# The last product of a decoder trunk: one half of the rows finished ahead of the other, with a norm and a way out for each half

## Chip, cores and metric

The kernel runs on one core of a Trainium2 chip. The metric is device microseconds (us) of one execution, lower is better; the number for a kernel is the median of its runs.

## What is computed

A decoder trunk of two layers over 256 positions of 2048 features, all float32. Only the end bears on this case: the last feed-forward's down projection, the residual, and the final norm.

```
gu = h @ w_gu;  gate, up = gu[..., :5632], gu[..., 5632:]
x = x + (silu(gate) * up) @ w_down          # w_down: 5632 x 2048
out = x * rsqrt(mean(x * x, axis=-1) + 1e-6) * norm_final
```

The root and its reciprocal are one number for each of the 256 rows.

## The kernel before

**Weights.** All weight matrices come as one stream of blocks of 128 x 1024 float32 (512 KB), in the order of use. `emit_dma` (L122) loads a block into one of five buffers (`wraw`) from SyncE's queue. `emit_split` (L130) writes it as the sum of two float32r halves: ScalarE copies it to `whi` (L134), VectorE subtracts that from it to get `wlo` (L135); there are three buffers of each. `next_block` (L148) hands out the next block and keeps the halving up to three blocks and the loads up to five blocks ahead in the written order.

**A wide product.** `wide_gemm` (L201) multiplies 256 rows by 512 columns of weights. A block holds two chunks of 128 x 512. The rows come in two halves, t = 0 (rows 0..127) and t = 1 (rows 128..255), each with an accumulator (`acc`) of its own in PSUM. For each chunk k and each half there are three matmuls: activation high by weight high (L211), high by low (L212), low by high (L213). The down projection has 44 chunks, so 22 blocks, for each of four column groups j.

**Residual and squares.** `residual` (L693) adds the accumulator to `xs`, the resident x (L698, VectorE, 128 x 512 a half), and squares it with a row sum into `ssq` (L701, ScalarE). In the last feed-forward GpSimd multiplies the finished columns by the final norm's gain for j = 0, 1, 2 (L705); for j = 3 the gain is multiplied in at the very end.

**Final norm.** `row_scale` (L680) sums the squares of both halves together (L685), takes the root on ScalarE (L686), and on VectorE the reciprocal with one correction step (L688 to L691). Then L831 to L836 multiply the eight 128 x 512 tiles by the row factor, VectorE for t = 0 (L835) and for the last columns of both (L831), ScalarE for t = 1 (L833). Each tile goes out with a transfer of 256 KB of its own, all eight from SyncE's queue (L836).

**Tables.** ScalarE's root and Silu are in different activation tables; a table is loaded where the next function in ScalarE's order needs one that is not there. The last Silu (L735) is in the last feed-forward's gate product.

**Order.** The order of the instructions on each engine is fixed when the program is built, by a planner. It plays the program through by its own costs: an instruction becomes free to go when its inputs are there and its buffers are free, and an engine takes, of those that are free to go, the one that was written first. The code as written is therefore no list of the order on an engine.

Of the kernel before, what the change touches and what calls it, by code (L numbers as in the profile page):

```python
# [11 lines left out]
F32 = mybir.dt.float32  # L12
F32R = mybir.dt.float32r
AF = mybir.ActivationFunctionType
OP = mybir.AluOpType
AX = mybir.AxisListType

P = 128
D = 2048
S = 256  # L20
# [12 lines left out]
EPS = 1e-6  # L33
# [12 lines left out]
N5 = 512  # L46
NJ = D // N5
# [15 lines left out]
def nsa_pool_trunk(ctx, tc, xT, xn, gain0, small, band, gfin, w_kc, w_qk, w_vg, w1k, w1v, w_o,  # L63
                   p_in, p_grp, p_out, gu, down, out):
    nc = tc.nc
# [5 lines left out]
    tmp = ctx.enter_context(tc.tile_pool(name="tmp", bufs=2))  # L71
# [3 lines left out]
    RAW, SPL = 5, 3  # L75
# [62 lines left out]
    def ahead(b):  # L138
        while state["split"] < min(len(stream), b + SPL):
            while state["dma"] <= state["split"]:  # L140
                emit_dma(state["dma"])
                state["dma"] += 1
            emit_split(state["split"])
            state["split"] += 1
        while state["dma"] < min(len(stream), b + RAW):
            emit_dma(state["dma"])
            state["dma"] += 1

    def next_block():
        b = state["used"]  # L150
        ahead(b)
        state["used"] += 1
        return parts.pop(b)


    def bank(own=False):

        i = state["acc"]
        state["acc"] += 1
        if state["more"] is None or own or i % state["turn"] == 0:  # L160
            return mm.tile([P, 512], F32, name="acc")
        return state["more"].tile([P, 512], F32, name="acc")
# [35 lines left out]
                k += 1  # L198
        return ps

    def wide_gemm(rhs, own=False):  # L201

        ps = [bank(own) for _ in range(2)]
        n = len(rhs)
        for k in range(n):
            if k % 2 == 0:
                w = next_block()
            hi, lo = (a[:, k % 2 * N5:(k % 2 + 1) * N5] for a in w)
            for t in range(2):
                xa, xb = (rhs[k][:, a * S + t * P:a * S + (t + 1) * P] for a in range(2))  # L210
                nc.tensor.matmul(ps[t], xa, hi, start=k == 0, stop=False)  # L211
                nc.tensor.matmul(ps[t], xa, lo, start=False, stop=False)  # L212
                nc.tensor.matmul(ps[t], xb, hi, start=False, stop=k == n - 1)  # L213
        return ps

    def whole(ps, name):

        t = tmp.tile([P, S], F32, name=name)
        nc.scalar.activation(t, ps[:, S:], AF.Copy)
        nc.vector.tensor_tensor(t, ps[:, :S], t, op=OP.add)  # L220
        return t
# [4 lines left out]
    eps = cst.tile([P, 1], F32, name="eps")  # L226

    def col(name, i=None, p=P):
        if name == "g_mix0":
            return g0[:, i:i + 1]  # L230
        a, b = COLS[name]
        return sm[:p, a:b] if i is None else sm[:p, a + i:a + i + 1]
# [10 lines left out]
    rcol = xgp.tile([P, 2], F32, name="rcol")  # L243
# [51 lines left out]
    with tc.tile_pool(name="first", bufs=1, reuse_waits="tile") as fp, \  # L295
# [5 lines left out]
        for b, n in enumerate(KB):  # L301
            x = x2[k0 // 2]
# [19 lines left out]
        k = 0  # L322
        for n in KB:
            hi, lo = next_block()
            for i in range(n):
                for j in range(3):
                    o = (3 * i + j) * P
# [30 lines left out]
        for j in range(2):  # L358
            ps = whole(gemm2(xg), "up").rearrange("p (c i k) -> p i c k", i=CS // 2, k=2)
            f = rst.rearrange("p (c i k) -> p i c k", i=CS // 2, k=2)  # L360
            for g in range(2):
                a = slice(g * DV, (g + 1) * DV)
# [12 lines left out]
        for u in range(2):  # L375

            t = fp.tile([P, KQ, 3, G, CS], F32, name="kab", bufs=2)
            w = col("posk")[:, u * CS:(u + 1) * CS].rearrange("p (m j) -> p m j", j=4)
# [4 lines left out]
            for j in range(3):  # L383
                r = slice(32 * j, 32 * j + 32)
# [3 lines left out]
            t = t.rearrange("p m j g c -> p (m j) g c")  # L388
            kab.append(halves(t, [P, 3 * KQ, G, CS], f"kab{u}"))
            t = fp.tile([P, CS // 2, G, CS], F32, name="vab", bufs=2)  # L390
            w = col("posv")[:, u * CS // 2:(u + 1) * CS // 2]
# [6 lines left out]
        for br in range(2):  # L398
# [4 lines left out]
            for u in range(2):  # L403
                o = CS + u * S + br * P
# [104 lines left out]
    op = ctx.enter_context(ExitStack())  # L509
# [4 lines left out]
    bias = {}  # L514
# [130 lines left out]
    for q in range(NH // 4):  # L645
# [3 lines left out]
        for j in range(3):  # L649
            ps = gemm(xg)  # L650
# [3 lines left out]
        for h in range(4 * q, 4 * q + 4, 2):  # L654
# [7 lines left out]
            o = oT[h // 2]  # L662
# [5 lines left out]
    xp = ctx.enter_context(tc.tile_pool(name="xp", bufs=1, reuse_waits="tile"))  # L668
# [1 line left out]
    state["turn"] = 3  # L670
    psT = ctx.enter_context(tc.tile_pool(name="psT", bufs=2, space=bass.MemoryType.PSUM))
    xs = xp.tile([P, 2, D], F32, name="xs")
    ssq = xp.tile([P, 2, NJ], F32, name="ssq")
    for t in range(2):
        nc.sync.dma_start(xs[:, t], xn[t * P:(t + 1) * P, :])

    def turn():
        return psT.tile([P, 2 * S], F32, name="turn")

    def row_scale():  # L680

        tot = tmp.tile([P, 2], F32, name="tot")
        a = tmp.tile([P, 2], F32, name="na")
        t = tmp.tile([P, 2], F32, name="nt")
        nc.vector.tensor_reduce(tot, ssq, axis=AX.X, op=OP.add)  # L685
        nc.scalar.activation(t, tot, AF.Sqrt, scale=1.0 / D, bias=eps)  # L686
        nc.vector.tensor_scalar(a, tot, 1.0 / D, EPS, op0=OP.mult, op1=OP.add)
        nc.vector.reciprocal(rcol, t)  # L688
        nc.vector.scalar_tensor_tensor(t, rcol, -0.5, rcol, op0=OP.mult, op1=OP.mult)
        nc.vector.tensor_tensor(t, t, a, op=OP.mult)  # L690
        nc.vector.scalar_tensor_tensor(rcol, t, 1.5, rcol, op0=OP.add, op1=OP.mult)  # L691

    def residual(j, ps, gain, gf=None):  # L693


        xc = [xs[:, t, j * N5:(j + 1) * N5] for t in range(2)]
        for t in range(2):
            nc.vector.tensor_tensor(xc[t], ps[t], xc[t], op=OP.add)  # L698
        for t in range(2):
            sq = xp.tile([P, N5], F32, name="sq", bufs=2)  # L700
            nc.scalar.activation(sq, xc[t], AF.Square, accum_out=ssq[:, t, j:j + 1])  # L701
        if gf is not None:
            if j < NJ - 1:
                for t in range(2):
                    nc.gpsimd.tensor_tensor(xc[t], xc[t], gf[j], op=OP.mult)  # L705
            return
        for q in range(2):
            tr = turn()
            for i in range(2):
                for t in range(2):  # L710
                    o = (2 * q + i) * P
                    nc.tensor.transpose(tr[:, i * S + t * P:i * S + (t + 1) * P], xc[t][:, o:o + P],  # L712
                                        ident)
            for i in range(2):
                spread(4 * j + 2 * q + i, tr[:, i * S:(i + 1) * S], gain)
# [11 lines left out]
    def ffn(gain, fpool):  # L727
        hid2, hid = pairs(fpool, FT, "hid")
        for f in range(FJ):
            pg = wide_gemm(xg)  # L730
            if f == 0:
                row_scale()
            sg = [fpool.tile([P, N5], F32, name=f"sg{t}", bufs=1) for t in range(2)]
            for t in range(2):
                nc.scalar.activation(sg[t], pg[t], AF.Silu, scale=rcol[:, t:t + 1])  # L735
            pu = wide_gemm(xg)
            h = [fpool.tile([P, N5], F32, name="h", bufs=4) for t in range(2)]
            for t in range(2):
                nc.vector.scalar_tensor_tensor(h[t], pu[t], rcol[:, t:t + 1], sg[t], op0=OP.mult,
                                               op1=OP.mult)  # L740
            for q in range(2):
                tr = turn()
                for i in range(2):
                    for t in range(2):
                        o = (2 * q + i) * P
                        nc.tensor.transpose(tr[:, i * S + t * P:i * S + (t + 1) * P],  # L746
                                            h[t][:, o:o + P], ident)
                split_pair(hid2[2 * f + q], tr)
        gf = None
        if gain is None:  # L750
            gf = [fpool.tile([P, N5], F32, name="h", bufs=4) for _ in range(NJ)]
            for j in range(NJ):
                nc.sync.dma_start(gf[j], gfin[:, j * N5:(j + 1) * N5])
        for j in range(NJ):
            residual(j, wide_gemm(hid), gain, gf)
        return gf

    for j in range(NJ):
        residual(j, wide_gemm(oT, own=j == 0), "g_ffn0")
# [6 lines left out]
    with tc.tile_pool(name="pl", bufs=1, reuse_waits="tile") as pl:  # L766
# [52 lines left out]
        rhs = [mixed[4 * g + c] for g in GROUPS for c in range(4)]  # L819
# [1 line left out]
            residual(j, wide_gemm(rhs), "g_ffn1")  # L821

    with tc.tile_pool(name="f1", bufs=1, reuse_waits="tile") as fpool:
        gf = ffn(None, fpool)
        row_scale()
        for j in (*range(NJ - 1), NJ - 1):
            for t in range(2):
                o = xs[:, t, j * N5:(j + 1) * N5]
                r = rcol[:, t:t + 1]
                if j == NJ - 1:  # L830
                    nc.vector.scalar_tensor_tensor(o, o, r, gf[j], op0=OP.mult, op1=OP.mult)  # L831
                elif t:
                    nc.scalar.activation(o, o, AF.Copy, scale=r)  # L833
                else:
                    nc.vector.tensor_scalar(o, o, r, None, op0=OP.mult)  # L835
                nc.sync.dma_start(out[t * P:(t + 1) * P, j * N5:(j + 1) * N5], o)  # L836


def _buckets():
# [118 lines left out]
```

## Time and profile before

| what | value |
|---|---|
| median of 3 runs | 2144.52 us |
| lowest and highest run | 2143.55, 2146.86 us |
| the profiled execution: its own time | 2141.8 us |
| its span, first to last instruction | 2139.6 us |
| TensorE busy | 2113.2 us, 99% of the span |
| VectorE, ScalarE, GpSimd busy | 55%, 48%, 3% |
| mean granted TensorE clock | 0.998 |

The profiled execution's time stands 2.2 us above its span. Times in the rows below are microseconds from the first instruction. TensorE's last matmul starts at 2125.85 us; what comes after it is the tail that the change works on.

### The profile page before, as it was taken

How to read it: one execution, taken by the hardware profiler on the slowest of the kernel's cores; microseconds unless marked ns; L12 is line 12 of the kernel's file. 1: busy time of each engine (PE TensorE's matmuls, PEld its weight loads, DVE VectorE, ACT ScalarE, POOL GpSimd, SP SyncE). 2: the span in 40 equal slices, each digit the busy share in tenths (PEclk: the TensorE clock that was granted, in tenths of full speed). 3: DMA queues.
4: the chain of work that ended last, by engine and by line, in shares of the span. 5: the costliest groups of instructions: out<-in, count | busy, mean ns of one | idle time of the engine just before them, and what ended most of it. 6: DMA issues, size and time to landing. Idle time of an engine off the chain costs nothing.

```text
span 2139.6 us, 28065 instructions
## 1 busy us (share of the span) xinstructions
PE 2113.2 (99%) x10780; PEld 1803.5 (84%) x10780; DVE 1181.9 (55%) x1527; ACT 1035.2 (48%) x1481; POOL 73.3 (3%) x135
## 2 busy tenths in 40 slices
PE   8999999999999999999999999999999999999997
PEld 7899999888888888888888888888888888888886
DVE  7768888555554545544444555555444554444443
ACT  5667777454444444444444455444444444444443
POOL 4001111000000000000000000000000000000000
PEclk9999999999999999999999999999999999999999
DMA  7664444666666666666666656666666666666664
GB/s 235 200 218 136 146 139 136 199 180 194 190 187 188 188 194 188 186 192 192 191 193 188 198 175 184 182 191 186 189 190 193 188 187 189 192 208 195 191 194 128
DMA packets 115720, 396.91 MB, mean 186 GB/s; under 512 B 13539, under 2 KB 19939, under 8 KB 115331
## 3 DMA queue, kind: packets, MB, share of 16 engines
q1 hardware_dynamic: 115538, 395.07, 62.1%
q8 instruction: 84, 1.38, 0.3%
q14 instruction: 50, 0.40, 0.1%
q10 hardware_dynamic: 48, 0.07, 0.0%
HBM read 391.25 MB, written 2.16 MB: 184 GB/s over the span
## 4 chain that ended last, share of the span: by engine, by line
PE 93%; DVE 0%; ACT 0%; DVEq 0%; issue 0%
PE acc L212 27%; PE acc L211 27%; PE acc L213 27%; PE acc L166 2%; PE acc L168 2%; PE acc L167 2%; PE turn L746 1%; PE ps_o L639 1%; PE ps_t L601 1%; PE ps_s L535 1%; PE ps_s L533 1%; PE ps_s L534 1%; PE turn L712 0%; PE ps_o L630 0%; PE ps_o L629 0%; PE ps_o L631 0%
## 5 line engine op out<-in xcount | busy, mean ns | idle before, releaser
L135 DVE TENSOR_TENSOR wlo<-wraw,whi 128x1024 fp32r<-128x1024 f32 (+1 forms) x727 | 886.9, 1221 | 855.8 <-ACT whi L134 849.0
L134 ACT ACTIVATE whi<-wraw 128x1024 fp32r<-128x1024 f32 (+1 forms) x727 | 765.6, 1053 | 924.6 <-PE acc L213 850.1
L213 PE MATMUL acc<-whi,xg 128*128 128x512 f32 x1536 | 599.8, 390 | 0.0
L212 PE MATMUL acc<-wlo,xg 128*128 128x512 f32 x1536 | 598.3, 390 | 0.0
L211 PE MATMUL acc<-whi,xg 128*128 128x512 f32 x1536 | 545.8, 390 | 0.0
L212 PEld LDWEIGHTS acc<-wlo,xg 128*128 128x128 f32 x1536 | 288.4, 188 | 59.2
L213 PEld LDWEIGHTS acc<-whi,xg 128*128 128x128 f32 x1536 | 288.4, 188 | 59.2
L211 PEld LDWEIGHTS acc<-whi,xg 128*128 128x128 f32 x1536 | 288.5, 188 | 58.5
L212 PE MATMUL acc<-wlo,hid 128*128 128x512 f32 x704 | 274.2, 390 | 0.0
L213 PE MATMUL acc<-whi,hid 128*128 128x512 f32 x704 | 274.1, 389 | 0.0
L211 PE MATMUL acc<-whi,hid 128*128 128x512 f32 x704 | 247.4, 390 | 0.0
L212 PEld LDWEIGHTS acc<-wlo,hid 128*128 128x128 f32 x704 | 132.1, 188 | 27.4
L211 PEld LDWEIGHTS acc<-whi,hid 128*128 128x128 f32 x704 | 132.2, 188 | 27.3
L213 PEld LDWEIGHTS acc<-whi,hid 128*128 128x128 f32 x704 | 132.2, 188 | 27.1
L166 PE MATMUL acc<-xg,whi 128*128 128x256 f32 x432 | 124.3, 289 | 6.1 <-ACT whi L134 5.8
L167 PE MATMUL acc<-xg,whi 128*128 128x256 f32 x432 | 123.2, 287 | 0.0
L168 PE MATMUL acc<-xg,wlo 128*128 128x256 f32 x432 | 121.5, 288 | 0.7 <-DVE wlo L135 0.6
L166 PEld LDWEIGHTS acc<-xg,whi 128*128 128x128 f32 x432 | 82.8, 192 | 6.9 <-ACT whi L134 6.3
L167 PEld LDWEIGHTS acc<-xg,whi 128*128 128x128 f32 x432 | 83.0, 192 | 0.0
L168 PEld LDWEIGHTS acc<-xg,wlo 128*128 128x128 f32 x432 | 81.5, 192 | 1.5 <-DVE wlo L135 1.1
L561 ACT ACTIVATE prob<-prob,mx 128x128 f32<-128x128 f32 (+1 forms) x128 | 56.6, 445 | 9.8 <-DVE mx L555 6.8
L212 PE MATMUL acc<-wlo,oT 128*128 128x512 f32 x128 | 50.8, 396 | 0.0
(211 smaller groups left out, 1876.1 us busy)
## 6 DMA issues: line engine op xcount, KB each, us to landing
wraw<-in_gu SPq DMA_DIRECT2D x352, 512.0 KB, 3.7
wraw<-in_down SPq DMA_DIRECT2D x176, 512.0 KB, 3.7
wraw<-in_w_qk SPq DMA_DIRECT2D x64, 512.0 KB, 4.3
wraw<-in_w_o SPq DMA_DIRECT2D x32, 512.0 KB, 3.7
wraw<-in_p_in SPq DMA_DIRECT2D x32, 512.0 KB, 3.6
wraw<-in_p_out SPq DMA_DIRECT2D x32, 512.0 KB, 3.6
bias<-skew SPq DMA_DIRECT2D x32, 200.0 KB, 3.3
wraw<-in_p_grp SPq DMA_DIRECT2D x8, 512.0 KB, 3.8
```

Source lines behind the costliest of these rows:

```text
L134: nc.scalar.activation(hi[:, :n], t[:, :n], AF.Copy)
L135: nc.vector.tensor_tensor(lo[:, :n], t[:, :n], hi[:, :n].bitcast(F32), op=OP.subtract)
L166: nc.tensor.matmul(ps, hi, x[:, :S], start=first, stop=False)
L167: nc.tensor.matmul(ps, hi, x[:, S:], start=False, stop=False)
L168: nc.tensor.matmul(ps, lo, x[:, :S], start=False, stop=last)
L211: nc.tensor.matmul(ps[t], xa, hi, start=k == 0, stop=False)
L212: nc.tensor.matmul(ps[t], xa, lo, start=False, stop=False)
L213: nc.tensor.matmul(ps[t], xb, hi, start=False, stop=k == n - 1)
L533: nc.tensor.matmul(o, q[0], k[0], start=True, stop=False)
L534: nc.tensor.matmul(o, q[0], k[1], start=False, stop=False)
L535: nc.tensor.matmul(o, q[1], k[0], start=False, stop=True)
L561: nc.scalar.activation(p[:, o:o + n], p[:, o:o + n], AF.Exp, bias=mx[:, i:i + 1], accum_out=su[:, i:i + 1])
```

## The change

`wide_gemm` gets an argument `apart`. The last `apart` chunks are written half by half: all their matmuls for t = 0, then all for t = 1. The last product of the program (j = 3 of the last down projection) is called with `apart=6`, three blocks. Those three blocks are asked for together, before the first of the 18 matmuls of t = 0.

`residual` and `row_scale` are no longer used for that last product. A new function `finish` does the residual, the squares, the norm and the output of one half; it is written for t = 0 and then for t = 1. The residual and the squares go in two pieces of 256 columns. The sum of the first three column groups and the first piece is taken apart from the last piece, and enters the root as its bias. ScalarE multiplies columns 0..1023 by the row factor in one instruction, VectorE the rest in two. Each half goes out in two transfers of 512 KB in place of four of 256 KB; the front columns of t = 1 go from ScalarE's queue, the others from SyncE's.

Ahead of the last down projection, behind the last Silu in the code, a root of one column that nobody reads is written, `root`. Its input is `eps`, a column made at the start (L238). `ssq` gets one more column.

```diff
-        for k in range(n):
+        def step(k, w, t):
+            hi, lo = (a[:, k % 2 * N5:(k % 2 + 1) * N5] for a in w)
+            xa, xb = (rhs[k][:, a * S + t * P:a * S + (t + 1) * P] for a in range(2))
+            nc.tensor.matmul(ps[t], xa, hi, start=k == 0, stop=False)
+            nc.tensor.matmul(ps[t], xa, lo, start=False, stop=False)
+            nc.tensor.matmul(ps[t], xb, hi, start=False, stop=k == n - 1)
+
+        for k in range(n - apart):
             if k % 2 == 0:
                 w = next_block()
...
             for t in range(2):
...
+                step(k, w, t)
+        ws = [next_block() for _ in range(apart // 2)]
+        for t in range(2):
+            for k in range(n - apart, n):
+                step(k, ws[(k - n + apart) // 2], t)
...
+            nc.scalar.activation(tmp.tile([P, 1], F32, name="root"), eps, AF.Sqrt)
-        for j in range(NJ):
+        for j in range(NJ - (gf is not None)):
             residual(j, wide_gemm(hid), gain, gf)
-        return gf
+        if gf is not None:
+            ps = wide_gemm(hid, apart=2 * SPL)
+            for t in range(2):
+                finish(t, ps[t], gf[NJ - 1])
+
+    def finish(t, ps, g):
+        h = N5 // 2
+        o = D - N5
+        x = xs[:, t]
+        for i in range(2):
+            a = x[:, o + i * h:o + (i + 1) * h]
+            nc.vector.tensor_tensor(a, ps[:, i * h:(i + 1) * h], a, op=OP.add)
+            sq = xp.tile([P, N5], F32, name="sq", bufs=2)
+            nc.scalar.activation(sq[:, :h], a, AF.Square, accum_out=ssq[:, t, NJ - 1 + i:NJ + i])
+        part, a, r, u = (xp.tile([P, 1], F32, name=f"{n}{t}") for n in ("part", "mean", "r", "u"))
+        last = ssq[:, t, NJ:]
+        nc.vector.tensor_reduce(part, ssq[:, t, :NJ], axis=AX.X, op=OP.add)
+        nc.vector.tensor_scalar(part, part, 1.0 / D, EPS, op0=OP.mult, op1=OP.add)
+        nc.scalar.activation(u, last, AF.Sqrt, scale=1.0 / D, bias=part)
+        nc.vector.tensor_scalar(a, last, 1.0 / D, part, op0=OP.mult, op1=OP.add)
+        nc.vector.reciprocal(r, u)
+        nc.vector.scalar_tensor_tensor(u, r, -0.5, r, op0=OP.mult, op1=OP.mult)
+        nc.vector.tensor_tensor(u, u, a, op=OP.mult)
+        nc.vector.scalar_tensor_tensor(r, u, 1.5, r, op0=OP.add, op1=OP.mult)
+        rows = out[t * P:(t + 1) * P]
+        nc.scalar.activation(x[:, :D // 2], x[:, :D // 2], AF.Copy, scale=r)
+        (nc.scalar if t else nc.sync).dma_start(rows[:, :D // 2], x[:, :D // 2])
+        nc.vector.tensor_scalar(x[:, D // 2:o], x[:, D // 2:o], r, None, op0=OP.mult)
+        nc.vector.scalar_tensor_tensor(x[:, o:], x[:, o:], r, g, op0=OP.mult, op1=OP.mult)
+        nc.sync.dma_start(rows[:, D // 2:], x[:, D // 2:])
...
-        gf = ffn(None, fpool)
-        row_scale()
...
+        ffn(None, fpool)
```

## Rows read from the trace of the kernel before

**Rows 1.** From the page: busy time, share of the span and instructions of each engine.

```profile
PE 2113.2 (99%) x10780; PEld 1803.5 (84%) x10780; DVE 1181.9 (55%) x1527; ACT 1035.2 (48%) x1481; POOL 73.3 (3%) x135
```

**Rows 2.** The chain that ended last, in order of time, from the last products to the end of the compute engines' work (start us, us, what).

```profile
2125.33 0.24 PE acc L213
...
2125.59 0.70 DVE xs L698
...
2126.32 1.40 ACT sq L701 x4
...
2127.74 1.28 ACT L686
...
2129.36 0.18 DVE rcol L688
...
2130.22 0.49 DVE xs L835
...
2131.50 1.33 DVE xs L831 x2
```

**Rows 3.** Timeline of TensorE in the last product: the start of the third block from the end, and the ends of the last halves (start us, us, engine, line, operation, tiles, count; consecutive instructions of one line are merged).

```profile
2117.91 0.62 PE L211 MATMUL acc<-whi,hid 128*128 128x512 f32 x2
2118.37 0.39 PE L212 MATMUL acc<-wlo,hid 128*128 128x512 f32 x1
...
2124.49 0.39 PE L213 MATMUL acc<-whi,hid 128*128 128x512 f32 x1
...
2125.17 0.39 PE L213 MATMUL acc<-whi,hid 128*128 128x512 f32 x1
...
2125.85 0.39 PE L213 MATMUL acc<-whi,hid 128*128 128x512 f32 x1
```

**Rows 4.** Timeline of ScalarE, then of VectorE, from 2113 us on: the last halving of a block on each, and on VectorE the one two blocks earlier as well.

```profile
2118.11 1.06 ACT L134 ACTIVATE whi<-wraw 128x1024 fp32r<-128x1024 f32 x1 [1.66 <-PE acc L213]
...
2113.77 1.23 DVE L135 TENSOR_TENSOR wlo<-wraw,whi 128x1024 fp32r<-128x1024 f32 x1 [1.49 <-ACT whi L134]
...
2119.21 1.23 DVE L135 TENSOR_TENSOR wlo<-wraw,whi 128x1024 fp32r<-128x1024 f32 x1 [1.49 <-ACT whi L134]
```

**Rows 5.** The way out: the instructions of the output's line (durations min/median/max in ns, first and last start) with the time from issue to landing; then stretches of the tail (stretch, its length, PE, PEld, DVE, ACT and POOL busy, PEclk, share of the DMA engines busy, GB/s).

```profile
L836 SPq DMA_DIRECT2D out_x<-xs x8: 344/480/598, 2130.7 to 2134.6; - x8
...
DMA to landing us min/median/max: 2.4/3.7/4.3
...
2132.00:2133.00 1.00, 0.00 (x0) 0.00 (x0) 0.82 (x2) 0.16 (x1) 0.00 (x0) 0.50 1.03 381
...
2131.60:2137.90 6.30, 0.00 (x0) 0.00 (x0) 1.23 (x2) 0.56 (x1) 0.00 (x0) 0.50 1.02 328
2137.90:2138.50 0.60, 0.00 (x0) 0.00 (x0) 0.00 (x0) 0.00 (x0) 0.00 (x0) 0.50 0.09 34
```

**Rows 6.** ScalarE's groups by shape (line, engine, operation, tiles, count | busy us, mean ns | idle before): the final root's table loads and activations; then the instructions of the line of Silu (durations, first and last start).

```profile
L686 ACT ACT_TABLE_LOAD x3 | 3.8, 1283 | 0.1
...
L686 ACT ACTIVATE nt<-tot,eps 128x2 f32<-128x2 f32 x4 | 1.2, 297 | 0.3 <-DVE tot L685 0.2
...
L735 ACT ACTIVATE sg<-acc,rcol x44: 682/690/692, 477.1 to 1864.2; 128x512 f32<-128x512 f32 x44
L735 ACT ACT_TABLE_LOAD  x2: 1283/1283/1283, 475.8 to 1418.0; - x2
```

**Rows 7.** Where early instructions stand: GpSimd's timeline from the start, ScalarE's from the start, and ScalarE's about 458 us, between attention's output product and the first feed-forward.

```profile
0.88 1.06 POOL L342 MEMSET v0h<- 128x1152 f32 x1
...
3.97 0.29 POOL masks.py:199 TENSOR_SCALAR_AFFINE_SELECT ident<-ident 128x128 f32<-128x128 f32 x1
...
2.03 0.20 ACT L238 ACTIVATE eps<-ones 128x1 f32<-128x1 f32 x1
3.58 0.51 ACT L247 ACTIVATE xg<-x,g 128x256 fp32r<-128x256 f32 x1 [1.35 <-DMA x<-in_xT]
...
26.09 1.28 ACT L261 ACT_TABLE_LOAD   x1
...
458.31 0.30 ACT L686 ACTIVATE nt<-tot,eps 128x2 f32<-128x2 f32 x1
...
460.28 0.84 ACT L247 ACTIVATE xg<-turn,sm 128x256 fp32r<-128x256 f32 x2 [0.73 <-PE turn L712]
```

**Rows 8.** Groups by shape of ScalarE and of VectorE that carry prices (columns as in the groups of ScalarE above).

```profile
L134 ACT ACTIVATE whi<-wraw 128x1024 fp32r<-128x1024 f32 x706 | 748.3, 1060 | 918.0 <-PE acc L213 850.1 <-PE acc L167 31.3 <-ACT xg L247 8.7
...
L651 ACT ACTIVATE q<-acc 128x256 fp32r<-128x256 f32 x24 | 8.7, 367 | 0.0
...
L652 DVE TENSOR_TENSOR q<-acc,q 128x256 fp32r<-128x256 f32 x24 | 9.8, 413 | 0.3 <-ACT q L651 0.3
...
L831 DVE SCALAR_TENSOR_TENSOR xs<-xs,rcol,h 128x512 f32<-128x512 f32 x2 | 1.4, 746 | 0.0
...
L835 DVE TENSOR_SCALAR xs<-xs,rcol 128x512 f32<-128x512 f32 x3 | 1.3, 483 | 0.1
```

**Rows 9.** DMA issues of the whole span: tiles, queue, operation, count, KB each, median us from issue to landing.

```profile
vc<-vp SPq DMA_DIRECT2D x6, 15.0 KB, 2.1
...
skew<-rrow ACTq DMA_DIRECT2D x1, 66.0 KB, 4.7
```

**Rows 10.** One stretch at the start (columns as in the stretches of the tail).

```profile
25.00:30.00 5.00, 5.00 (x37) 4.42 (x37) 3.28 (x9) 3.64 (x4) 0.00 (x0) 1.00 0.76 258
```

More of the change, by code (lines that the diff above doesn't have):

```diff
@@ L199, in gemm2, with wide_gemm @@
         return ps
-    def wide_gemm(rhs, own=False):
+    def wide_gemm(rhs, own=False, apart=0):
         ps = [bank(own) for _ in range(2)]
         n = len(rhs)
-        for k in range(n):
+        def step(k, w, t):
[5 more added lines that the diff above has]
+        for k in range(n - apart):
             if k % 2 == 0:
                 w = next_block()
-            hi, lo = (a[:, k % 2 * N5:(k % 2 + 1) * N5] for a in w)
             for t in range(2):
[L210 to L213, printed above, removed]
+                step(k, w, t)
[3 more added lines that the diff above has]
+                step(k, ws[(k - n + apart) // 2], t)
         return ps
@@ L672, in nsa_pool_trunk @@
     xs = xp.tile([P, 2, D], F32, name="xs")
-    ssq = xp.tile([P, 2, NJ], F32, name="ssq")
+    ssq = xp.tile([P, 2, NJ + 1], F32, name="ssq")
     for t in range(2):
@@ L684, in row_scale @@
         t = tmp.tile([P, 2], F32, name="nt")
-        nc.vector.tensor_reduce(tot, ssq, axis=AX.X, op=OP.add)
+        nc.vector.tensor_reduce(tot, ssq[:, :, :NJ], axis=AX.X, op=OP.add)
         nc.scalar.activation(t, tot, AF.Sqrt, scale=1.0 / D, bias=eps)
@@ L702, in residual @@
         if gf is not None:
-            if j < NJ - 1:
-                for t in range(2):
-                    nc.gpsimd.tensor_tensor(xc[t], xc[t], gf[j], op=OP.mult)
+            for t in range(2):
+                nc.gpsimd.tensor_tensor(xc[t], xc[t], gf[j], op=OP.mult)
             return
@@ L753, in ffn @@
                 nc.sync.dma_start(gf[j], gfin[:, j * N5:(j + 1) * N5])
-        for j in range(NJ):
+            nc.scalar.activation(tmp.tile([P, 1], F32, name="root"), eps, AF.Sqrt)
+        for j in range(NJ - (gf is not None)):
             residual(j, wide_gemm(hid), gain, gf)
-        return gf
+        if gf is not None:
+            ps = wide_gemm(hid, apart=2 * SPL)
+            for t in range(2):
+                finish(t, ps[t], gf[NJ - 1])
[24 more added lines that the diff above has]
+        nc.sync.dma_start(rows[:, D // 2:], x[:, D // 2:])
     for j in range(NJ):
@@ L823, in nsa_pool_trunk @@
     with tc.tile_pool(name="f1", bufs=1, reuse_waits="tile") as fpool:
-        gf = ffn(None, fpool)
-        row_scale()
[L826 to L836, printed above, removed]
+        ffn(None, fpool)
 def _buckets():
```

## The prediction

> **What bounds the kernel now.** I read the page's busy shares first: TensorE works 2113.2 of 2139.6 us, so outside a head and a tail no engine but TensorE has time to give [rows 1]. The change adds and removes no matmul, so I went to the tail, in the chain of waits: the reader is to see that the last matmul product hands over at 2125.6 and that from there to 2139.6 everything stands in one line: two adds and squares, a table load of 1.28 us, the root, the factor, the scaling, the way out [rows 2]. Then the way out by stretches: the eight transfers are issued from 2130.74 to 2134.6, and the DMA engines are full from 2131.6 to 2137.9 at 328 GB/s; the last bytes move by 2138.5 [rows 5]. So the end is set by the time at which the first of 2.10 MB can go, and by the rate. All that the change can win lies in these 14 us, 0.65% of the time. Last I read the order of the instructions in the timelines, because the change works only if it is also the order on the engines.
>
> The profiled execution took 2141.8 us, 2.2 us over its span, and lies 2.7 us under the median of 2144.52. I make sums against its span and take the difference off the median.
>
> **Part 1, the apart chunks.** As written, the 18 matmuls of rows 0..127 come first. The third block from the end begins at 2117.91; one matmul takes (2125.85 - 2117.91) / 35 = 0.227 us [rows 3]. The first half would then end at 2117.91 + 17 x 0.227 + 0.39 = 2122.16 instead of 2125.56. The last weights would be in time: their low part is there at 2119.21 + 1.23 = 2120.44 [rows 4] and is wanted at 2120.86.
>
> I don't think that this is the order that runs. At the start of each block the trace has L211 twice, then L212 [rows 3]; written is L211, L212, L213 of one half, then the other half. The other half's L211 has been drawn ahead of an L212 whose low weights, on the chip, were there since 2113.77 + 1.23 = 2115.00 [rows 4], 2.9 us before the block began. So in the planner's reckoning a block's weights come only just when the block begins, in every block of the stream, and TensorE fills with what is free to go. With the change, the planner finds after the six matmuls of the first half on one block that the next block isn't there, and takes the six of the second half. The order is then six and six, block by block, and the first half ends six matmuls before the end: 2124.49 + 0.39 = 2124.88 [rows 3], 0.68 us earlier than now. TensorE's own time is the same either way, no wait is added: cost nothing, cover the 2.72 us of a block's matmuls against 1.06 and 1.23 us of halving.
>
> **Part 2, root's table.** The load of 1.28 us stands in the chain [rows 2]. The added root reads only `eps`, which is there at 2.2 us. What needs nothing runs early here: the clearing of `v0h`, written behind the whole first product, runs at 0.88, ahead of a step of the identity at 3.97; the first feed-forward's root, written behind its first product, runs at 458.31, ahead of the spreads at 460.28 that are written before it [rows 7]. ScalarE idles 1.35 us ahead of 3.58 [rows 7]. So I expect the added root there, some 1860 us ahead of the last Silu. Silu then takes the table: the four roots of L686 have three loads, the one without having no Silu ahead of it since the last, and Silu's 44 instructions have two loads, one behind each feed-forward's root [rows 6]. The first half's root then still pays 1.28 us, the second half's not. At the head load and root take 1.28 + 0.30 of 1.35 us idle, 0.2 us over; in return the load at 26.09 falls away [rows 7], where TensorE is busy 5.00 of 5.00 us [rows 10] and wins nothing. I take zero, between 0.25 lost and 0.2 won.
>
> **Part 3, `finish`, by the order of part 1.** No row has a square of 256 columns: between 0.34 (half of 0.68 for 512, two of them in 1.40 [rows 2]) and 0.68. Copies go from 1.060 at 1024 to 0.367 at 256 columns [rows 8], 0.9 ns a column, so 0.68 - 0.23 = 0.45. Adds of 256 columns take 0.41 [rows 8].
> - First half: adds 2124.91 to 2125.74, squares to 2126.27, table to 2127.55, root 0.30 to 2127.85. From the reciprocal to the first scaling it is 2130.22 - 2129.36 = 0.86 [rows 2]: factor at 2128.7. VectorE scales in 0.48 + 0.75 [rows 8] to 2129.95; ScalarE's 1024 columns (1.06) come out at 2129.8 to 2130.2, behind the other half's squares. The extra small VectorE steps (0.17 each) fit under the squares and the load.
> - Second half: adds 2126.27 to 2127.1; its squares are queued behind the table load and the root on ScalarE, 2127.85 to 2128.8; its root at 2128.8 or, behind the first half's copy, 2130.2; its factor, also behind the first half's scaling on VectorE, at 2130.8 to 2131.3; scaled by 2131.9 to 2132.5.
>
> **Part 4, the way out.** Four issues take the place of eight; the first goes at 2129.95 instead of 2130.74. The first half's 1.05 MB at 328 GB/s last 3.2 us, until 0.9 + 3.2 us later, 2134.05; the second half's transfers are queued by 2132.5, so the engines never starve, and the end moves by the start alone: 0.8 us. Rows of 4 KB instead of 2 KB have no price here: the rate may stay 328 or reach the 381 of the best full microsecond [rows 5], 0.9 us more; I take 328, which is of the same tensor and direction. The sum: 0 + 0 + 0.8, span 2138.8, forecast 2144.5 - 0.8 = 2143.7.
>
> The trace has 7.6 us from the first issue, 2130.74, to the last landing, 2134.6 + 3.7 [rows 5]. The Trainium skill, page "DMA: Bandwidth & Descriptors", section "Anatomy of one DMA", gives 2.0 us plus the bytes at 436 GB/s for one transfer, an estimate of 6.8 us here. By that the end would be at 2129.95 + 6.8 + 1.3 = 2138.05 and the time 2143.0; the measured row decides.
>
> **The rivals.**
> - *The table holds, the order is six and six.* If the planner leaves the added root behind Silu, the first half's root is done at 2126.57 and its first transfer goes at 2128.65: 2.1 us won, 2142.4. For it: the place in the code; against it, the early steps of [rows 7].
> - *Both as written.* First half: factor at 2122.19 + 0.83 + 0.53 + 0.30 + 0.86 = 2124.7, transfers at 2125.95, landed before the others start. Second half: adds from 2126.27, squares to 2127.6, root 2127.9, factor 2128.8, both transfers at 2130.0. Then only 1.05 MB is left: 2130.0 + 0.9 + 3.2, and from the full stretch's end to the span's end 1.7 as now [rows 5]: 2135.8, 3.8 us won, 2140.7; at 381 GB/s 2140.3. Against it: L211 twice in each block [rows 3].
> - *Order as written, table not held.* The first half's factor at 2126.0; if its scaling stands ahead of the second half's adds on VectorE, these start at 2127.25 instead of 2126.27: 2.8 us won, 2141.7.
> - *Slower: ScalarE's queue.* The front columns of the second half leave from it. Its only transfer in this trace, 66 KB, landed after 4.7 us, 15 KB from SyncE after 2.1 [rows 9]. If the 2.6 us between them go with the number of rows, 32 there and 128 here, it lands after 2.1 + 10.4 = 12.5 us: 2131.9 + 12.5 + 1.3 = 2145.7, 6.1 us lost, 2150.6. It decides from a landing of 6.4 us on. Against it: the 66 KB were issued among weight loads, with the DMA engines 0.76 busy [rows 10]. The Trainium skill, same page, section "Issuing engines are not separate DMA queues", has all queues on the same 16 engines; by that rule this rival is out and 2143.7 stands. No run here shows it yet.
>
> **How the numbers follow.** A measurement of this kernel can tell about 0.2%, 4.3 us, from no change. Chances: forecast 0.56, table held alone 0.14, both as written 0.10, written order without the table 0.12, ScalarE's queue 0.05, something else 0.03. None of the four that win reaches 4.3 us by its sum; both as written at the better rate comes to 4.25, so half of its chance is faster, and with the scatter of runs for the rest faster is 0.10. Slower: 0.05 and 0.03 of scatter, 0.08. Within 0.2%: 0.82. The range goes down to 2140.2, both as written at the better rate, and up to 2146.2: no gain, 0.9 us lost to the head, to late copies or to a poorer rate, and a median that lies 0.8 us off (the three runs lie 3.3 us apart).
>
> **What would show it.** Right: in the last three blocks six matmuls of one half, then six of the other; a root of one column on ScalarE before 4 us; a table load of 1.28 us about 2126.3 between the first half's squares and its root; the first transfer issued near 2130 and full DMA engines until about 2137. Wrong: 18 matmuls of one half in a row, a root behind 1864 us that nobody waits for and none in the tail with a load, a gap in the transfers between the halves, the last issue before 2130.5. The forecast is wrong if the span changes by over 2 us either way.

## The result: 17 us slower, and not in the tail

The changed kernel takes 2161.06 us (median of 4 runs, 2159.3 to 2162.7) against 2144.03 for the kernel before (4 runs): 1.0079 times, with an interval of 1.0067 to 1.0091. Ratios here and below come from the single runs of both kernels, so they need not be the quotient of the two medians shown; the 95% interval stands in brackets. Forecast was 2143.7.

The first thing to read is what the page says of the engines, against [rows 1]:

```profile
PE 2131.8 (99%) x10780; PEld 1805.1 (84%) x10780; DVE 1181.9 (55%) x1536; ACT 1035.6 (48%) x1486; POOL 73.6 (3%) x135
```

TensorE ran the same 10780 matmuls and was busy 18.6 us longer. VectorE and ScalarE were not. So the loss is in the matmuls themselves. TensorE's groups by shape of the kernel before (line, operation, tiles, count | busy us, mean ns of one | idle before):

```profile
L212 PE MATMUL acc<-wlo,xg 128*128 128x512 f32 x1536 | 598.3, 390 | 0.0
L212 PE MATMUL acc<-wlo,hid 128*128 128x512 f32 x704 | 274.2, 390 | 0.0
L213 PE MATMUL acc<-whi,hid 128*128 128x512 f32 x704 | 274.1, 389 | 0.0
...
L212 PE MATMUL acc<-wlo,oT 128*128 128x512 f32 x128 | 50.8, 396 | 0.0
...
L212 PE MATMUL acc<-wlo,mixed 128*128 128x512 f32 x128 | 50.1, 392 | 0.0
```

and the same groups after (its lines are one lower, L211 for L212):

```profile
L211 PE MATMUL acc<-wlo,xg 128*128 128x512 f32 x1536 | 598.3, 390 | 0.0
...
L211 PE MATMUL acc<-wlo,hid 128*128 128x512 f32 x704 | 279.3, 397 | 0.0
L212 PE MATMUL acc<-whi,hid 128*128 128x512 f32 x704 | 279.2, 397 | 0.0
...
L211 PE MATMUL acc<-wlo,mixed 128*128 128x512 f32 x128 | 51.0, 398 | 0.0
L211 PE MATMUL acc<-wlo,oT 128*128 128x512 f32 x128 | 50.8, 397 | 0.0
```

The reader is to see that one shape of matmul has two durations, and that the activation's tile decides which. With `xg` it is 390 ns in both kernels. With `hid` (2112 matmuls) and `mixed` (384) it went from 390 to 397. With `oT` (384) it was 397 all along, which I had passed over. Seven ns for 2496 matmuls are 17.5 us, nearly all of the 18.6. The pace shows it too: VectorE halves one block for every 12 matmuls, every 2.72 us before,

```profile
1991.37 1.23 DVE L135 TENSOR_TENSOR wlo<-wraw,whi 128x1024 fp32r<-128x1024 f32 x1 [1.49 <-ACT whi L134]
1994.09 1.23 DVE L135 TENSOR_TENSOR wlo<-wraw,whi 128x1024 fp32r<-128x1024 f32 x1 [1.49 <-ACT whi L134]
```

and every 2.81 us after, with as much more idle time on VectorE, so VectorE waits and does not set the pace:

```profile
1990.71 1.23 DVE L135 TENSOR_TENSOR wlo<-wraw,whi 128x1024 fp32r<-128x1024 f32 x1 [1.59 <-ACT whi L134]
1993.53 1.23 DVE L135 TENSOR_TENSOR wlo<-wraw,whi 128x1024 fp32r<-128x1024 f32 x1 [1.59 <-ACT whi L134]
```

The mean granted clock is 0.997 after and 0.998 before, and the slow products begin with the first feed-forward, 1100 us ahead of any instruction of the last product. Neither explains a loss in some products alone.

**The tail** itself got shorter, as forecast. From the last matmul's start to the end of the span it is 2157.0 - 2143.81 = 13.2 us; before it was 13.75 [rows 1, 3]. ScalarE's timeline at the start, then in the tail, then the queues' issues, all of the changed kernel:

```profile
2.26 1.28 ACT L763 ACT_TABLE_LOAD   x1
3.56 0.20 ACT L763 ACTIVATE root<-eps 128x1 f32<-128x1 f32 x1
3.66 0.49 ACT L256 ACTIVATE xg<-x,g 128x256 fp32r<-128x256 f32 x1
...
2143.53 0.42 ACT L780 ACTIVATE sq<-xs 128x256 f32<-128x256 f32 x1 [6.66 <-DVE xs L778]
...
2145.18 0.40 ACT L780 ACTIVATE sq<-xs 128x256 f32<-128x256 f32 x1
...
2145.69 1.28 ACT L785 ACT_TABLE_LOAD   x1
2146.98 0.48 ACT L785 ACTIVATE u<-ssq,part 128x1 f32<-128x1 f32 x2
2148.21 2.19 ACT L792 ACTIVATE xs<-xs,r 128x1024 f32<-128x1024 f32 x2 [0.75 <-DVE r L790]
...
2149.38 0.34 SPq L793 DMA_DIRECT2D out_x<-xs  x1
2149.78 1.24 SPq L796 DMA_DIRECT2D out_x<-xs  x2
...
2150.43 0.40 ACTq L793 DMA_DIRECT2D out_x<-xs  x1
```

The added root stands at 3.56 us, and the table load is still in the tail, behind the squares of both halves.

### The profile page after: what moved, and what is told of

Same layout as the page of the kernel before. It is cut to its first block, busy times and chain, and to the rows that moved or that the text cites. A ratio compares the mean times of both kernels' runs of the same rounds, so it can differ in the third digit from the quotient of the medians.

```text
span 2157.0 us, 28079 instructions
## 1 busy us (share of the span) xinstructions
PE 2131.8 (99%) x10780; PEld 1805.1 (84%) x10780; DVE 1181.9 (55%) x1536; ACT 1035.6 (48%) x1486; POOL 73.6 (3%) x135
## 4 chain that ended last, share of the span: by engine, by line
PE 93%; DVE 0%; ACT 0%; DVEq 0%; issue 0%; ACTq 0%
PE acc L210 27%; PE acc L212 27%; PE acc L211 27%; PE acc L166 2%; PE acc L168 2%; PE acc L167 2%; PE turn L754 1%; PE ps_o L648 1%; PE ps_t L610 1%; PE ps_s L544 1%; PE ps_s L542 1%; PE ps_s L543 1%; PE turn L720 0%; PE ps_o L639 0%; PE ps_o L640 0%; PE ps_o L638 0%
## 5 line engine op out<-in xcount | busy, mean ns | idle before, releaser
L212 PE MATMUL acc<-whi,xg 128*128 128x512 f32 x1536 | 599.7, 390 | 0.0
L211 PE MATMUL acc<-wlo,xg 128*128 128x512 f32 x1536 | 598.3, 390 | 0.0
L210 PE MATMUL acc<-whi,xg 128*128 128x512 f32 x1536 | 545.7, 390 | 0.0
L211 PEld LDWEIGHTS acc<-wlo,xg 128*128 128x128 f32 x1536 | 288.4, 188 | 59.4
L212 PEld LDWEIGHTS acc<-whi,xg 128*128 128x128 f32 x1536 | 288.4, 188 | 59.1
L210 PEld LDWEIGHTS acc<-whi,xg 128*128 128x128 f32 x1536 | 288.5, 188 | 58.3
L211 PE MATMUL acc<-wlo,hid 128*128 128x512 f32 x704 | 279.3, 397 | 0.0
L212 PE MATMUL acc<-whi,hid 128*128 128x512 f32 x704 | 279.2, 397 | 0.0
L210 PE MATMUL acc<-whi,hid 128*128 128x512 f32 x704 | 252.5, 397 | 0.0
L212 PEld LDWEIGHTS acc<-whi,hid 128*128 128x128 f32 x704 | 132.6, 188 | 32.1
L211 PEld LDWEIGHTS acc<-wlo,hid 128*128 128x128 f32 x704 | 132.6, 188 | 32.1
L210 PEld LDWEIGHTS acc<-whi,hid 128*128 128x128 f32 x704 | 132.6, 188 | 32.0
L211 PE MATMUL acc<-wlo,mixed 128*128 128x512 f32 x128 | 51.0, 398 | 0.0
```

## The experiments

A profile doesn't show where tiles lie, but the built program does. Offsets in a partition, in bytes modulo 256, with the pace per block of 12 matmuls that each run then gave. `hid` and `mixed` share one offset; `whi` and `wlo` share one.

| kernel | weights | xg | hid, mixed | oT | pace with xg | with hid | with oT |
|---|---|---|---|---|---|---|---|
| before | 192 | 192 | 192 | 224 | 2.72 | 2.72 | 2.80 |
| after | 192 | 192 | 32 | 224 | 2.72 | 2.81 | 2.80 |
| e1, e7 | 192 | 192 | 64 | 224 | 2.72 | 2.79 | 2.80 |
| e2 | 192 | 192 | 224 | 224 | 2.72 | 2.80 | 2.80 |
| e3 | 192 | 192 | 0 | 224 | 2.72 | 2.80 | 2.80 |
| f1 | 224 | 224 | 224 | 224 | 2.72 | 2.72 | 2.72 |
| f2 | 224 | 192 | 192 | 224 | 2.80 | 2.80 | 2.72 |
| g1, g2, g4, g5 | 192 | 192 | 192 | 224 | 2.72 | 2.72 | 2.80 |
| h1, g3 | 192 | 192 | 192 | 192 | 2.72 | 2.72 | 2.72 |

The change moves `hid` by 352 bytes (122304 to 122656) with tiles that nobody would count: `root` takes 2 x 32 bytes in its pool, the wider `ssq` goes from 32 to 64, and the eight columns of `finish` take 8 x 32. All lie ahead of `hid`.

Theory A is that the place of an operand in SBUF sets a matmul's time; first I thought that it must be a multiple of 64 bytes. Theory B is that something which the change does at run time slows these products: the early root and its table, or the other order. Theory C is that any later address costs. Four runs came first.

**e1: after, with `hid` on a multiple of 64.**

```diff
-    ssq = xp.tile([P, 2, NJ + 1], F32, name="ssq")
+    ssq = xp.tile([P, 2, NJ + 5], F32, name="ssq")[:, :, :NJ + 1]
```

> The changed kernel with 32 bytes a partition more in the tile of ssq, nothing else; hid, pooled and mixed then begin at a multiple of 64 bytes again, as in the kernel before. Theory A (the 17 us are matmuls that read the activations, their stationary operand, from an address 32 bytes off a multiple of 64; 2112 with hid and 384 with mixed at 0.234 instead of 0.227 us): the pace of the last product is back at 0.227, a block in 2.72 us, and only the tail's gain is left, so 2143 to 2144 us, 0.3 to 0.8 us under before. Theory B (the early root has changed the order or the timing of the whole program): it stays at 2161 us. Theory C (a later address as such costs, since more bytes lie ahead): 2161 or a little more.

Measured: 2156.06 us against 2143.06, 1.0057 [1.0044, 1.0069]; pace with `hid` 2.79. That is about 5 us better than the changed kernel and still 13 us over before, so the multiple of 64 is wrong.

**e2: before, with the one column alone.**

```diff
-    ssq = xp.tile([P, 2, NJ], F32, name="ssq")
+    ssq = xp.tile([P, 2, NJ + 1], F32, name="ssq")
...
-    nc.vector.tensor_reduce(tot, ssq, axis=AX.X, op=OP.add)
+    nc.vector.tensor_reduce(tot, ssq[:, :, :NJ], axis=AX.X, op=OP.add)
```

> The kernel before with the one column more of ssq and nothing else of the change; the tile grows from 32 to 64 bytes and hid begins 32 bytes off a multiple of 64. Theory A: the whole loss from this alone, 2161 us, 17 us over before, hid's matmuls at 0.234 us. Theory B: 2144 us, since neither the order nor the root is touched. Theory C (any later address): 2161 us as well.

Measured: 2158.3, 1.0068 [1.0055, 1.0081]. One unread column, which moves `hid` by 32 bytes, costs nearly what the whole change cost. The groups of e2:

```profile
L212 PE MATMUL acc<-wlo,xg 128*128 128x512 f32 x1536 | 598.2, 389 | 0.0
L212 PE MATMUL acc<-wlo,hid 128*128 128x512 f32 x704 | 278.8, 396 | 0.0
...
L212 PE MATMUL acc<-wlo,mixed 128*128 128x512 f32 x128 | 50.9, 397 | 0.0
```

No root, no apart chunks and no `finish` are in e2, so theory B is not the cause of these 15 us.

**e3: before, with five more columns** (`NJ + 5` in e2's place).

> The kernel before with five columns more of ssq; the tile grows by 64 bytes, so hid begins later than in the run with one column, but at a multiple of 64. Theory A: 2144 us, no change. Theory C (a later address as such): 2161 us or more. Theory B: 2144 us.

Measured: 2156.92, 1.0067 [1.0054, 1.0079], pace 2.80. Here `hid` lies on a multiple of 256 and is as slow, so that place is not good by itself either. Theory C is still open.

**e7: after, e1's tile, and both parts of the change held to the order written.** The planner is told to keep the added root, and the matmuls of the last six chunks, where they are written:

```diff
-            nc.scalar.activation(tmp.tile([P, 1], F32, name="root"), eps, AF.Sqrt)
+            tc.keep_in_program_order(nc.scalar.activation(tmp.tile([P, 1], F32, name="root"), eps, AF.Sqrt))
...
+            pin = tc.keep_in_program_order if k >= n - apart else (lambda i: i)
-            nc.tensor.matmul(ps[t], xa, hi, start=k == 0, stop=False)
+            pin(nc.tensor.matmul(ps[t], xa, hi, start=k == 0, stop=False))
...
```

> The changed kernel, aligned as in the first run, and its order held to what is written: the root stays behind Silu, the 36 last matmuls run 18 for one half and 18 for the other. If the tail's account of the prediction holds, both as written win 3.8 us over before: 2140 to 2140.7 us, no table load in the tail, the first half's transfers issued about 3.3 us behind its last matmul and landed before the other half's, 10 us from the last matmul's start to the end of the span instead of 13.75. If the way out is bound by something other than the bytes (the landing of two transfers, the ends of the queues): 2142 us or more. Theory B for the 17 us would leave it at 2157 us.

Measured: 2152.46, 1.0041 [1.0027, 1.0054]. The tail is 2152.5 - 2143.13 = 9.4 us. The change's intention is worth 4.4 us there, and the matmuls' pace still takes more than that away.

**The new theory.** In the kernel before, `oT` is the one operand that lies elsewhere modulo 256 than the weights, and the one that is slow. So A in its second form (theory D in the expectations): what counts is the distance between the stationary operand (activations) and the moving operand (weights) modulo 256 bytes; at 0 a matmul of the wide products takes 389 to 392 ns, elsewhere 394 to 398 (the high by high line of `oT`, which also waits for its operand, lies at 401 and, where `oT` is fast, at 396). Its rival (theory E) is that certain places are slow whatever the weights do. The next two runs move the weights.

**f1: before, everything on the left side 32 bytes later.**

```diff
+    cpad = cst.tile([P, 8], F32, name="cpad")
+    nc.vector.memset(cpad, 0.0)
     sm = cst.tile([P, NSMALL], F32, name="sm")
```

> The kernel before with a tile of 32 bytes ahead of all others; weights, xg, hid and mixed all begin 32 bytes later, oT, which is laid out from the other end, stays. The runs so far left out a multiple of 64 as the rule: the products with hid and mixed are slow at addresses of 0, 32, 64 and 224 modulo 256 and fast at 192, which is also where the weights' buffers begin; xg is at 192 and always fast, oT at 224 and always slow. Theory D (what counts is the distance between the activations, stationary, and the weights, moving, modulo 256): all products stay at 2.72 us a block, and attention's output product, oT now at 224 like the weights, comes down from 2.80 to 2.72, 32 blocks: about 2.6 us less than before, 2140.5 us. Theory E (the stationary operand's own address counts): every product is slow, 384 blocks with xg as well, some 45 us more, 2190 us.

Measured: 2141.13 against 2143.73, 0.9986 [0.9977, 0.9995]. `hid` lies at 224 as in e2, and `oT` at 224 as before, and now both are fast, because the weights lie there too:

```profile
L212 PE MATMUL acc<-wlo,hid 128*128 128x512 f32 x704 | 274.3, 390 | 0.0
...
L212 PE MATMUL acc<-wlo,mixed 128*128 128x512 f32 x128 | 50.1, 392 | 0.0
L212 PE MATMUL acc<-wlo,oT 128*128 128x512 f32 x128 | 50.1, 391 | 0.0
```

**f2: before, the weights alone 32 bytes later against `xg`, `hid` and `mixed`.**

```diff
     nc.vector.memset(ones, 1.0)
+    cpad = cst.tile([P, 8], F32, name="cpad")
+    nc.vector.memset(cpad, 0.0)
...
+    xpad = xgp.tile([P, 56], F32, name="xpad")
+    nc.vector.memset(xpad, 0.0)
     xg = [xgp.tile([P, 2 * S], F32R, name=f"xg{c}") for c in range(KC)]
```

> The kernel before with 32 bytes ahead of the weights' buffers and 224 more ahead of xg; the weights begin at 224 modulo 256, xg, hid and mixed at 192 as before, 256 bytes later. Theory D: 384 blocks with xg, 176 with hid and 32 with mixed go from 2.72 to 2.80 us, 47 us more, oT's 32 come down, 2.6 us less: 2187 us. Theory E: 2143 us, no change. A theory that any change of the layout costs (the kernel before had a lucky one) has 2157 us.

Measured: 2185.72, 1.0194 [1.018, 1.0208]. Now `xg`, never slow until here, is slow, and `oT` alone is fast:

```profile
L212 PE MATMUL acc<-wlo,xg 128*128 128x512 f32 x1536 | 606.6, 395 | 0.0
...
L212 PE MATMUL acc<-wlo,hid 128*128 128x512 f32 x704 | 278.3, 395 | 0.0
...
L212 PE MATMUL acc<-wlo,oT 128*128 128x512 f32 x128 | 50.2, 392 | 0.0
```

f1 and f2, set against before and e2, are the proof. `hid` at 224 is slow in e2 and fast in f1; `xg`, `hid` and `mixed` at 192 are fast in before and slow in f2; `oT` at 224 is slow in before and fast in both. What decides is where the weights lie, so theory E falls. f1 also has `hid` later than before and fast, so theory C falls too, and g1 below has it 512 bytes later. A period of 512 bytes does not fit: from `whi` (41152 in before) `hid` lies 317 x 256 bytes away and `xg` (65728) 96 x 256, an odd and an even multiple, and both are fast.

The same runs limit the finding. In other products the weights are the stationary operand and `xg` the moving one, in matmuls of 128x256. Those are no slower at a distance of 32 bytes, here in before and then in f2:

```profile
L167 PE MATMUL acc<-xg,whi 128*128 128x256 f32 x432 | 123.2, 287 | 0.0
...
L167 PE MATMUL acc<-xg,whi 128*128 128x256 f32 x432 | 123.6, 288 | 0.0
```

**g1: after, with `hid` back at 192** (e1's edit with `NJ + 24`, 160 bytes more).

> The changed kernel with 160 bytes more in the tile of ssq than it has; hid, pooled and mixed begin at 192 modulo 256, as in the kernel before. Theories D and E: the products are at 2.72 us a block, and the tail alone is left, with 13.2 instead of 13.75 us from the last matmul's start to the end of the span: 0.5 us under before, which a comparison of runs can't tell from no change. If any change of the layout costs: 2156 us.

Measured: 2142.47 against 2143.73, 0.9994 [0.9985, 1.0003]. This is the change as I had costed it, with the pace of before, and it lies 0.06% under, which the runs can't tell from no change; the forecast was 0.04% under. The tail is 2142.8 - 2129.62 = 13.2 us, as in after.

**g2: g1 with both parts held** (e7's edit).

> As the run before this one, and the order held to what is written: the root behind Silu, the last 36 matmuls 18 and 18. Theories D and E: 2.72 us a block and the tail of the earlier run with both held, which was 10.1 us from the last matmul's start to the end of the span where the kernel before has 13.75: 3.6 us under before, 2139.5 us, a ratio of 0.9983. If any change of the layout costs: 2152 us.

Measured: 2138.54, 0.9979 [0.997, 0.9988]; the tail is 2138.8 - 2129.41 = 9.4 us. ScalarE and the queues in its tail:

```profile
2126.94 0.19 ACT L781 ACTIVATION_READ_ACCUMULATOR sq<-xs 128x1 f32 x1
2127.20 0.29 ACT L786 ACTIVATE u<-ssq,part 128x1 f32<-128x1 f32 x1
2128.36 1.15 ACT L793 ACTIVATE xs<-xs,r 128x1024 f32<-128x1024 f32 x1 [0.87 <-DVE r L791]
2130.29 0.42 ACT L781 ACTIVATE sq<-xs 128x256 f32<-128x256 f32 x1 [0.77 <-DVE xs L779]
...
2129.55 0.34 SPq L794 DMA_DIRECT2D out_x<-xs  x1
2129.94 4.02 SPq L797 DMA_DIRECT2D out_x<-xs  x2
...
2133.62 0.39 ACTq L794 DMA_DIRECT2D out_x<-xs  x1
```

No table load stands ahead of the root, and the first half's transfers go out at the time of the last matmul.

**g4 and g5: g1 with one part held, the root in g4, the matmuls in g5.**

> The changed kernel, aligned, with the root held behind Silu and the order of the matmuls left to the planner. The tail loses the load of 1.28 us that stands between the squares of both halves and their roots: 13.2 - 1.3 = 11.9 us from the last matmul's start to the end, 1.9 us under before (the prediction's sum for this case was 2.1). If the load was hidden behind the second half's way: 13.2 us.

> The changed kernel, aligned, with the last 36 matmuls held 18 and 18 and the root left to the planner, so the load stays in the first half's chain. The prediction's sum for this case: 2.8 us under before, the second half's adds 1 us behind their matmuls because VectorE still scales the first half; about 10.9 us of tail. If the load is covered by the second half's 4.1 us of matmuls: 9.4 us of tail, like the run with both held.

Measured: g4 2142.11 against 2143.18, 0.9996 [0.9987, 1.0005], tail 2139.9 - 2128.08 = 11.8 us. g5 2140.03, 0.9986 [0.9977, 0.9995], tail 2139.8 - 2129.60 = 10.2 us. In the tail the table is worth 13.2 - 11.8 = 1.4 us, the order 3.0, both together 3.8, less than their sum. In the time of a whole run g4's gain does not show (0.9996 beside 0.9994 for g1); it is read from the traces alone. g5's tail of 10.2 lies between its two expectations, 10.9 and 9.4. In g5 the first half pays the load, and that pushes the second half's adds on VectorE behind the first half's scaling (ScalarE's load, then VectorE, last row of the first half and first of the second):

```profile
2127.37 1.28 ACT L786 ACT_TABLE_LOAD   x1
...
2130.25 0.75 DVE L796 SCALAR_TENSOR_TENSOR xs<-xs,r,h 128x512 f32<-128x512 f32 x1
2130.91 0.75 DVE L779 TENSOR_TENSOR xs<-acc,xs 128x256 f32<-128x256 f32 x2
```

**h1 and g3: `oT` moved to 192 as well, in before (h1) and in g2 (g3).**

```diff
     oT = [o_pool.tile([P, 2 * S], F32R, name=f"oT{c}") for c in range(KC)]
+    opad = o_pool.tile([P, 1], F32, name="opad")
+    nc.vector.memset(opad, 0.0)
```

> The kernel before with 32 bytes more in the pool of oT and nothing else: oT at 192 modulo 256, like the weights. Theory D: attention's output product at 2.72 us a block instead of 2.80, 2.6 us under before, 2141 us, a ratio of 0.9988. If the distance didn't count but only the layout as a whole: no gain or a loss of some 15 us.

> The version with both held and hid and mixed at the weights' address modulo 256, and 32 bytes more in the pool of oT, so that attention's output product has its activations there too (192). By theory D its 32 blocks come from 2.80 to 2.72 us, as they did where the weights were moved to oT's address: 2.6 us on top of the 4.4 us that the run with both held won, 7 us under before, 2136 us, a ratio of 0.9967. If oT's own address counts (224 was fast in the shifted kernel): no more than 4.4 us.

Measured: h1 2140.12 against 2143.18, 0.9994 [0.9985, 1.0003], which by itself tells nothing; its trace has the products with `oT` at 392 ns and 2.72 us a block, and a span of 2137.4 against 2139.6:

```profile
L212 PE MATMUL acc<-wlo,oT 128*128 128x512 f32 x128 | 50.1, 392 | 0.0
L213 PE MATMUL acc<-whi,oT 128*128 128x512 f32 x128 | 49.9, 392 | 0.0
```

g3 takes 2136.98, 0.9976 [0.9967, 0.9985], with a tail of 2135.3 - 2125.93 = 9.4 us. It is the best version measured and beats both kernels; the runs can't tell it from g2, whose interval overlaps.

## Why the prediction was wrong

**The step that failed** is in part 1: "TensorE's own time is the same either way, no wait is added: cost nothing". TensorE's time was not the same: its last matmul started at 2143.81 us instead of 2125.85, 18 us later. The order did cost nothing, but I had costed the change's instructions and not its memory. No part of the prediction asks what the nine new columns and the wider `ssq` push aside, and no rival does. They moved the stationary operand of 2496 matmuls from distance 0 to a distance of 96 bytes modulo 256, 7 ns each. e2 shows the mechanism without the change, g1 the change without the mechanism. The trace of before did carry the sign: `oT` at 396 to 401 ns beside `xg` at 390, in one shape.

**What held, by its own steps.**
- Part 1, the order: the planner drew it block by block, as forecast. In each of the last three blocks the second half's first matmul was drawn in behind the first half's first, as in before (L210 twice below, the last two blocks of the changed kernel). So the first half's last matmul started 2143.81 - 2142.64 = 1.17 us ahead of the last one, five matmuls and not six:

```profile
2138.42 0.63 PE L210 MATMUL acc<-whi,hid 128*128 128x512 f32 x2
...
2141.24 0.63 PE L210 MATMUL acc<-whi,hid 128*128 128x512 f32 x2
...
2142.64 0.40 PE L212 MATMUL acc<-whi,hid 128*128 128x512 f32 x1
...
2143.81 0.39 PE L212 MATMUL acc<-whi,hid 128*128 128x512 f32 x1
```

- Part 2, the table: the root went to the start (3.56 us), the load stayed in the tail and the one at 26 us is gone [rows 7]. g4 shows that the early place is all that kept the load there: held, the root takes 1.4 us off the tail.
- Parts 3 and 4 came out near by their sum, about 0.5 us won in the tail for 0.8 forecast, but by luck, through two errors of opposite sign. The first transfer was to go at 2129.95, 4.1 us behind the last matmul's start; before it was 4.9 [rows 3, 5], and it came 2149.38 - 2143.81 = 5.6 behind it. The planner put the second half's squares ahead of the load: it stands 1.9 us behind the last matmul's start, where I had 0.4. Both halves' roots then ran together, and the first half's first transfer left only 1.05 us ahead of the second half's (2149.38 and 2150.43): hardly anything of one half finishing ahead was left. Against that, the way out was faster than the 328 GB/s that I took, and near the 381 that I had kept as the other end. The stretch after (length, five engines' busy time, PEclk, DMA share, GB/s), which answers to [rows 5]:

```profile
2150.10:2155.50 5.40, 0.00 (x0) 0.00 (x0) 0.33 (x1) 0.29 (x1) 0.00 (x0) 0.50 0.98 388
```

The same bytes took 5.4 us instead of 6.3. Whether the longer rows, the smaller number of transfers or the second queue did that was not separated. The 6.8 us that the prediction set beside its sum come from a fit that the Trainium skill, in the section cited there, gives for transfers issued by GpSimd; these leave from SyncE and ScalarE, and the sum did not use it.

**The rivals.** "Both as written" was priced at 3.8 us; held so, the tail is 13.75 - 9.4 = 4.4 us shorter. "The table holds" was priced at 2.1 and measures 13.75 - 11.8 = 1.9 in g4; "order as written" at 2.8 and measures about 3.5 (13.75 to 10.2) in g5. ScalarE's queue, the rival on the slower side, falls: the two transfers of the front columns, one from SyncE's queue and one from ScalarE's, land 2.7 and 4.3 us after their issue (the minimum and the maximum below), both under the 6.4 from which it was to decide:

```profile
DMA to landing us min/median/max: 2.7/3.5/4.3
```

The time was slower than before, but not by any mechanism that I had named.

**What stays open.** Why the distance matters was not found out. Tried were distances of 0, 32, 64, 96, 128 and 224 bytes modulo 256; only 0 was fast. Steps finer than 32 bytes weren't tried, nor were `whi` and `wlo` moved apart; `wraw`, from which they are made, has the weights' offset too and moved along in f1 and f2, so its part is not separated. Profiled executions also differ by up to 4 us in their first 150 us (in g2 the granted clock is 0.93 from 50 to 100 us, in before 1.00), which is why tails are measured here from the last matmul and not on the absolute clock.

## What to carry to other kernels

Cost a change's memory as well as its instructions: a new tile, however small, moves the tiles laid out behind it, and here 32 bytes cost 15 us (e2). If a trace shows one shape of instruction with two durations that go with an operand's tile, compare the operands' addresses before anything else. And a change whose gain rests on an order is measured only once the order is held; left to the planner, this one gave about 0.5 us of the tail's 4.4.

## What the runs showed of the hardware

- In the wide products here a float32r matmul of 128x128 by 128x512 follows the one before it after 0.227 us (2.72 for 12) when its stationary and moving operands lie at the same offset modulo 256 bytes, and after 0.232 to 0.234 us at the five other distances tried: 2 to 3% of such a product. Over the whole kernel that is the span from 2137.6 us (f1, every one fast) to 2183.4 (f2, only `oT` fast). Matmuls of 128x256 with the weights stationary took 287 ns at a distance of 0 (before) and 288 at 32 bytes (f2).
- The Trainium skill, page "SBUF — State Buffer", section "Operand start alignment", requires only that an operand start on a multiple of its element's size, and says that this is about legality and that its runs timed nothing. No run here tried a place that is not a multiple of 32 bytes. For speed the runs add that the place counts: 0.227 beside 0.234 us a matmul, as above.
- Four transfers of 512 KB on two queues moved 2.10 MB at 388 GB/s, eight of 256 KB on one queue at 328 [rows 5]; which of the differences did that is open.
